# A two-layer hybrid block with routed experts: the modulation's sums as TensorE products, a table in longer runs, and new estimates for the planner

## The chip, the core and the metric

The kernel runs on one core of one Trainium2 chip. The metric is the time of one execution in device microseconds (us), as the median of the runs shown. The core has a matrix engine (TensorE, PE in the rows; PEld is its weight load), VectorE (DVE), ScalarE (ACT), GpSimd (POOL) and SyncE (SP), which issues the DMAs of this kernel in the order of its queue. Each engine takes its instructions in the order in which the program has them, and waits on semaphores for the others.

## The reference

One layer is computed for 512 latent tokens and 256 context tokens of 1024 channels: a bidirectional gated delta rule with 8 heads, whose context states seed the latent scans, and then an expert-choice mixture of 16 experts. Shift, scale and gate of both parts come from a modulation row.

```python
c_act = jax.nn.silu(c)
mod = c_act @ w_mod[i] + b_mod[i]
sh_m, sc_m, gt_m, sh_f, sc_f, gt_f = jnp.split(mod, 6, axis=-1)
u = modulate(rmsnorm(h, norm_mix_g[i]), sh_m, sc_m)
...
y, yc = gated_deltanet(u, uc, ...)       # projections, convolutions, chunked delta rule
h = h + gt_m * y
h = h + gt_f * ec_moe(modulate(rmsnorm(h, norm_ffn_g[i]), sh_f, sc_f), ...)
return rmsnorm(h, final_g)
```

## The kernel before

**The front** computes the norms, the modulation and the mixer; **the expert part** then streams 403 MB of expert weights (`wgu`, `wd`, `wdt`) through a ring of 2 MB tiles, each of which is used by products as it lands.

In the front, all channels of the tokens lie on partitions (`uh`, `ul` are the two halves of a split of the input, so that a projection takes three products instead of one, L141 to L143). `bulk` projects the 31 items (v, q, k, z of each head) one behind the other on TensorE. Each head then goes through these steps, of which different heads are in work at the same time:

- `conv` (L283): five taps on VectorE and ScalarE.
- `head_a`: reads the decay table from DRAM into two tiles `ff` (L1060), masks them on GpSimd (L1065), and builds the matrix of a chunk, whose diagonal blocks go through DRAM to `invert`.
- `invert`: 31 steps of two GpSimd instructions (L1148, L1150) that invert 32 x 32 blocks of all chunks; the blocks come in with `lb<-bd`, the result goes out with `xd<-xb` (L1153) and comes back with `cr<-xd` (L1158).
- `head_b`: puts the whole inverse together from the blocks, products from L1227 to L1275 with copies on VectorE between.
- `scan`: six steps in each of two directions, each a chain of products (L1315, L1321, L1333) and copies on VectorE and ScalarE. `decay_q` reads the table again for the queries (L1290).
- `head_o` and the output projection (L457 to L459): 64 sums of three products, 192 in all, of two heads together where they are paired, each closed by an addition into `hres` (L475). Router and top-k follow.

**The modulation** has two parts. The first sixteen column blocks are needed at the start and are products with `cst`, the activation padded to 32 columns (`mod_rows`, L818). The other 32 pieces of 512 KB (`mods`, `mod_piece`) are loaded one after the other into two slots (`e<-in_wm`, L344). A piece is multiplied by the activation and summed over eight blocks on VectorE (L373, L375), or on GpSimd (L355, L364, L367), or on ScalarE with sums on one of the others (L360, L364, L367), by the letters of `MOD_E`; then a product with a matrix of ones sums over the partitions (L382, L396).

**The table** `grow_d` is written once by `gates` as 96 rows of 128 values, a row for each direction, chunk and head, and read by `grow` with every partition reading the same rows: six of 512 bytes for `ff`, four for the queries.

**The order** of the front is written by a planner that runs when the program is built. Every step is a generator that asks for an engine with an estimated duration (`Ask("V", 0.25, t)`); the planner keeps a time for each engine, takes the request that could begin first (a rank decides between those that could begin together), and adds `HOP` before the next step may use the result. `dma` estimates loads. The estimates set only the order of the instructions; at run time an engine waits for what it needs. `E_AT` holds the first weights back until that planned time, `MOD_STEP` is the planned distance of two modulation pieces.

Of the kernel before, what the change touches and what calls it, by code (L numbers as in the profile page):

```python
# [25 lines left out]
H = 8  # L26
# [23 lines left out]
def gdn_moe_kernel(ctx: ExitStack, tc: tile.TileContext, a, out):  # L50
# [109 lines left out]
    def dma(nbytes, at=0.0):  # L160

        dq[0] = max(dq[0], at + 0.7) + nbytes / 360e3
        return dq[0] + 1.1
# [75 lines left out]
    av = lambda n_: 0.1 + n_ * 0.00084  # L239
    dv = lambda n_: 0.08 + n_ * 0.00104  # L240
# [17 lines left out]
    def conv(nm, h, n_, parts, last):  # L258
# [8 lines left out]
        else:  # L267
# [10 lines left out]
            for j in range(5):  # L278
                t = yield Ask("VA"[j == 0], 1.06 * dv(w) if j else 1.11 * av(w), t)
# [67 lines left out]
    def mod_piece(n_, j, wm, wsl, t):  # L347

        t = yield Ask(None, 0.0, lambda: t if n_ < 2 else None if ("mm", n_ - 2) not in done else max(t, done["mm", n_ - 2]))
        if MOD_E[n_] != "V":  # L350
            if MOD_E[n_] == "G":
                for i in range(2):
                    t = yield Ask("G", 1.25, t)
                    hk = slice(4 * i, 4 * i + 4)
                    g.tensor_tensor(wm[:, hk], wm[:, hk], cs1[:, hk, 0:1].to_broadcast([P, 4, P]), OP.mult)  # L355
            else:
                for i in range(4):
                    t = yield Ask("A", 0.59, t)
                    for k in (2 * i, 2 * i + 1):
                        s.mul(wm[:, k], wm[:, k], cs1[:, k, 0:1])  # L360
            en, on = ("V", v) if MOD_E[n_] == "B" else ("G", g)
            for i in (4, 2):
                t = yield Ask(en, dv(P * i) if en == "V" else 0.25 + 0.27 * i, t)
                on.tensor_add(wm[:, :i], wm[:, :i], wm[:, i:2 * i])  # L364
            t = yield Ask(en, dv(P) if en == "V" else 0.5, t)
            acc = accs[n_ % 2]
            on.tensor_add(acc, wm[:, 0], wm[:, 1])  # L367
        else:
            acc = accs[n_ % 2]
            for k in range(KT):  # L370
                t = yield Ask("V", 0.25, t)
                if k == 0:
# [133 lines left out]

    def with_router(hT, sl2, t, dst):

        t = yield Ask("P", 0.72, t, "pq")
        sl = take("pq")  # L510
        pr = psum_tile(ps, [P, P], "pq", 3)
        for k in range(KT):
# [1238 lines left out]
```

## Time and profile before

| what | us |
|---|---|
| median of 3 runs | 1574.14 |
| lowest and highest | 1568.88, 1575.66 |
| the profiled execution, its own time | 1573.24 |
| its span, first to last instruction | 1571.5 |
| TensorE busy in the span | 1374.7 (87%) |
| VectorE, ScalarE, GpSimd busy | 721.5, 405.3, 381.0 |
| mean granted share of TensorE's clock | 0.958 |

The profile is of one execution. The windows give busy time of each engine in a stretch, with the number of records in brackets; a 4-byte product of the kernel's kind stands in the records twice, so sixteen records are eight products. A wait is put down to what ended last before the waiting instruction began. The chain of waits is followed back from the last instruction.

### The profile page before, as it was taken

Reading aid. Unit: us, or ns where it says so; the run is one execution under the profiler, and the core shown is the slowest. Engines: PE = TensorE matmul, PEld = TensorE weight load, DVE = VectorE, ACT = ScalarE, POOL = GpSimd, SP = SyncE. Lnnn points to the kernel's source line nnn. Section 1 sums busy time; section 2 is a strip of 40 time slices with the busy share of each in tenths; the row PEclk is TensorE's granted clock in tenths of the full one; section 3 lists DMA queues with packets and bytes.
Section 4 is the critical chain, followed back from the end, with each engine's and each line's share of the span. In section 5 each row is a group of like instructions: output and inputs, shape, how many; then the busy total and the mean of one; then the engine's idle time right before and its main releaser. Section 6 shows DMA issues by size and latency. Waiting matters only on the chain.

```text
span 1571.5 us, 20699 instructions
## 1 busy us (share of the span) xinstructions
PE 1374.7 (87%) x8058; PEld 752.6 (48%) x8058; DVE 721.5 (46%) x1545; ACT 405.3 (26%) x1038; POOL 381.0 (24%) x645
## 2 busy tenths in 40 slices
PE   5889898988986889999999989889889899899867
PEld 1677687766875766433434324224223323324314
DVE  7779896977995896222222222222222222222103
ACT  3356474655574533000000000000000000000012
POOL 2548866857657830000000000000000000000001
PEclk8889999999998999999999999999999999999979
DMA  8145443443453566899999999999999999999992
GB/s 347 54 135 142 135 114 91 117 130 95 133 122 72 205 243 248 364 426 426 425 426 425 425 426 426 427 425 425 426 425 426 426 425 426 425 426 426 425 426 109
DMA packets 112515, 480.12 MB, mean 306 GB/s; under 512 B 45505, under 2 KB 66209, under 8 KB 81826
## 3 DMA queue, kind: packets, MB, share of 16 engines
q1 hardware_dynamic: 112418, 478.81, 77.9%
q8 instruction: 63, 1.03, 0.3%
q14 instruction: 34, 0.28, 0.1%
HBM read 471.92 MB, written 6.86 MB: 305 GB/s over the span
## 4 chain that ended last, share of the span: by engine, by line
DMA 48%; PE 26%; DVE 14%; POOL 8%; issue 2%; ACT 1%; SPq 0%; DVEq 0%; POOLq 0%; ACTq 0%
DMA w<-in_wgu 25%; DMA w<-in_wd 13%; PE gu L1580 10%; PE dn L1561 4%; POOL xb L1150 3%; POOL tb L1148 3%; DMA cr<-xd 2%; DVE e L375 2%; PE gc L1561 2%; PE gc L1511 2%; DMA fg<-in_fg 1%; DVE wl L303 1%; DMA ff__690<-grow_d 1%; DMA ff__1139<-grow_d 1%; PE gc L1548 1%
## 5 line engine op out<-in xcount | busy, mean ns | idle before, releaser
L1580 PE MATMUL gu<-w,xsT 128*64 128x512 f32 x2044 | 472.9, 606 | 32.4 <-DMA w<-in_wgu 31.6
L1580 PEld LDWEIGHTS gu<-w,xsT 128*64 128x64 f32 x2044 | 138.4, 138 | 291.5 <-issue 239.4
L1667 POOL TENSOR_TENSOR hres<-acc,fg 128x256 f32<-128x256 f32 (+1 forms) x6 | 6.0, 1004 | 953.1 <-DVE acc L1655 953.0
L1561 PE MATMUL dn<-w,work 128*64 128x512 f32 x896 | 202.0, 600 | 25.2 <-DMA w<-in_wd 25.2
L1550 DVE TENSOR_TENSOR acc<-gc,acc 128x512 f32<-128x512 f32 x104 | 70.7, 690 | 299.5 <-PE gc L1548 299.5
L141 PE MATMUL pp<-uh,wh 128*128 128x512 f32 (+1 forms) x368 | 153.4, 417 | 1.7 <-ACT cz L265 1.7
L143 PE MATMUL pp<-uh,wl 128*128 128x512 f32 (+1 forms) x368 | 138.9, 377 | 3.8 <-DVE wl L303 2.9
L142 PE MATMUL pp<-ul,wh 128*128 128x512 f32 (+1 forms) x368 | 137.9, 375 | 0.0
L1561 PEld LDWEIGHTS dn<-w,work 128*64 128x64 f32 x896 | 62.4, 137 | 154.2 <-issue 116.8
L1148 POOL TENSOR_TENSOR tb<-lb,xb 96x126 f32<-96x126 f32 (+22 forms) x248 | 118.3, 477 | 65.8 <-DMA lb<-bd 48.6
L1150 POOL TENSOR_TENSOR xb<-xb,tb 96x126 f32<-96x126 f32 (+22 forms) x248 | 125.1, 504 | 19.4
L1532 ACT ACTIVATE work<-tr 128x512 f32<-128x512 f32 x14 | 8.4, 597 | 423.1 <-PE tr L1525 423.1
L1512 DVE TENSOR_SCALAR xsT<-gc,ffn 128x128 f32<-128x128 f32 x64 | 26.2, 410 | 154.1 <-PE gc L1511 154.1
L1542 ACT CAST yh<-work 64x512 fp32r<-64x512 f32 x28 | 17.3, 617 | 253.1 <-DVE work L1539 252.8
L143 PEld LDWEIGHTS pp<-uh,wl 128*128 128x128 f32 x368 | 74.7, 203 | 16.1 <-DVE wl L303 3.3
L141 PEld LDWEIGHTS pp<-uh,wh 128*128 128x128 f32 x368 | 75.1, 204 | 10.7 <-ACT cz L265 2.2
L142 PEld LDWEIGHTS pp<-ul,wh 128*128 128x128 f32 x368 | 75.3, 205 | 6.3
L1511 PEld LDWEIGHTS gc<-oneh,hres 128*128 128x128 f32 x512 | 64.5, 191 | 20.2 <-issue 18.3
L1511 PE MATMUL gc<-oneh,hres 128*128 128x128 f32 x512 | 69.2, 280 | 0.4 <-DVE oneh L1504 0.4
L375 DVE SCALAR_TENSOR_TENSOR e<-e,cs,e 128x128 f32<-128x128 f32 x133 | 66.0, 512 | 1.8
L1613 DVE TENSOR_TENSOR work<-gu,work 128x512 f32<-128x512 f32 x32 | 22.0, 692 | 80.9 <-PE gu L1580 79.7
L1548 PEld LDWEIGHTS gc<-yh,pgt 128*128 128x128 f32 x112 | 19.8, 186 | 82.0 <-issue 68.2
(443 smaller groups left out, 2042.7 us busy)
## 6 DMA issues: line engine op xcount, KB each, us to landing
w<-in_wgu SPq DMA_DIRECT2D x100, 2048.0 KB, 34.3
w<-in_wd SPq DMA_DIRECT2D x45, 2048.0 KB, 34.3
w<-in_wgu SPq DMA_DIRECT2D x55, 1024.0 KB, 31.9
w<-in_wd SPq DMA_DIRECT2D x22, 1024.0 KB, 31.8
e<-in_wm SPq DMA_DIRECT2D x32, 512.0 KB, 4.4
wt<-in_win SPq DMA_DIRECT2D x31, 512.0 KB, 4.6
w<-in_wdt SPq DMA_DIRECT2D x6, 2048.0 KB, 30.7
wm<-in_wm SPq DMA_DIRECT2D x3, 2048.0 KB, 14.6
```

What stands on the lines that cost most here:

```text
L141: pe.matmul(pp, wh[:, k, :], uh[i][:, k, :], start=k == 0, stop=False)
L142: pe.matmul(pp, wh[:, k, :], ul[i][:, k, :], start=False, stop=False)
L143: pe.matmul(pp, wl[:, k, :], uh[i][:, k, :], start=False, stop=k == KT - 1)
L375: v.scalar_tensor_tensor(acc, wm[:, k], cs1[:, k, 0:1], acc, op0=OP.mult, op1=OP.add)
L1148: g.tensor_tensor(t_, lb[:, k + 1:, k:k + 1].to_broadcast([2 * NB, m, n_]), xb[:, k:k + 1, 0:n_].to_broadcast([2 * NB, m, n_]), OP.mult)
L1150: g.tensor_tensor(xb[:, k + 1:, 0:n_], xb[:, k + 1:, 0:n_], t_, OP.subtract)
L1511: pe.matmul(pg, hres[:, t, k * P:k * P + P], oneh[:, t].rearrange("p a b -> p (a b)"), start=t == 0, stop=t == NC_LAT - 1)
L1512: v.tensor_scalar(xsT[:, k, :], pg, ffn[:, 0, k:k + 1], ffn[:, 1, k:k + 1], op0=OP.mult, op1=OP.add)
L1548: pe.matmul(pcb, pgt[:, t, :], yh[:, dh], start=True, stop=True)
L1550: v.tensor_add(acc[t // 2][:, t % 2, cs], pcb, hres[:, t, cs] if first else acc[t // 2][:, t % 2, cs])
L1561: pe.matmul(pd[64 * g_:64 * g_ + 64], hs_[g_][i][:, cb, 64 * j:64 * j + 64], wcols(w, c0, w_), start=ft == 0, stop=ft == 15, tile_position ...
L1580: pe.matmul(gu[m][f // 2][hs], xsT[:, k, es], wcols(w, 2048 * m + 512 * f, 512), start=k == 0, stop=k == KT - 1, tile_position=(0, 64 * (f ...
```

## The change

Three things are changed.

1. **Modulation.** `MOD_E` goes. Each of the 32 pieces is now computed as the first sixteen blocks are: eight products with `cst`, four of them side by side in strips of 32 rows, into one PSUM tile; ScalarE copies it, and the closing product sums the four strips with `sel` (one column) or `selb` (the same column repeated). `cst` moves to a pool that lives through the front.
2. **Table.** `grow_d` has a row of 768 values for each direction and head. It is written with two DMAs and read with one run of 3 KB (for `ff`) or 2 KB (for the queries) per partition.
3. **Estimates.** Nearly every duration of the planner, `HOP`, the estimate of a DMA, `E_AT` and `MOD_STEP` get other values. The order of all five engines changes with them.

```diff
-    HOP = {"P": 0.27, "A": 0.33, "V": 0.33, "G": 0.35, "D": 0.0, None: 0.0}
+    HOP = {"P": 0.2, "A": 0.06, "V": 0.06, "G": 0.08, "D": 0.0, None: 0.0}
-    E_AT = (410, 425)
+    E_AT = (440, 460)
-    MOD_STEP = 7
-    MOD_E = "GGAGVVVVGVBVAVAVVVVVAVGAVVVVBVGV"
+    MOD_STEP = 11
-    def dma(nbytes, at=0.0):
-        dq[0] = max(dq[0], at + 0.7) + nbytes / 360e3
-        return dq[0] + 1.1
+    def dma(nbytes, at=0.0, more=0.0):
+        dq[0] = max(dq[0], at + 0.3) + nbytes / 380e3 + more
+        return dq[0] + 1.3
...
-                    t = yield Ask("G", 1.25, t)
-                    g.tensor_tensor(wm[:, hk], wm[:, hk], cs1[:, hk, 0:1].to_broadcast([P, 4, P]), OP.mult)
...
-            on.tensor_add(acc, wm[:, 0], wm[:, 1])
...
-                    v.scalar_tensor_tensor(acc, wm[:, k], cs1[:, k, 0:1], acc, op0=OP.mult, op1=OP.add)
-        give(wsl, t + 1.0)
+        t = yield Ask("P", 0.46, lambda: ..., "pq")
+        pm = psum_tile(ps, [P, P], "pq", 3)
+        for k in range(KT):
+            q = 32 * (k % 4)
+            pe.matmul(pm[q:q + 32, :], cst[:, k, :], wm[:, k, :], start=k < 4, stop=k >= 4)
+        give(wsl, t)
+        t = yield Ask("A", 0.27, t)
+        acc = accs[n_ % 2]
+        s.copy(acc, pm)
-        t = yield Ask("P", 0.15, t + 3.0, "pq")
+        t = yield Ask("P", 0.14, t, "pq")
-            pe.matmul(pc, acc, ones[:, 0:1], start=True, stop=True)
+            pe.matmul(pc, acc, sel[:, 0:1], start=True, stop=True)
-            pe.matmul(pb[hs], ones[:, hs], acc, start=True, stop=True)
+            pe.matmul(pb[hs], selb[:, hs], acc, start=True, stop=True)
...
-    grow_d = tc.dram_tile([2 * NCH * H, C], F32, name="grow_d")
+    grow_d = tc.dram_tile([2 * H, NCH * C], F32, name="grow_d")
-        sy.dma_start(grow_d, gr)
+        for d in range(2):
+            sy.dma_start(grow_d[d * H:(d + 1) * H].rearrange("h (c i) -> c h i", c=NCH), gr[d * NCH * H:(d + 1) * NCH * H])
-        return bass.AP(tensor=grow_d.tensor, offset=grow_d.offset + ((d * NCH + c) * H + h) * C,
-                       ap=[[0, P], [H * C, NCH - c], [1, C]])
+        return bass.AP(tensor=grow_d.tensor, offset=grow_d.offset + ((d * H + h) * NCH + c) * C,
+                       ap=[[0, P], [1, (NCH - c) * C]])
...
-                t = yield Ask("V", 0.26, t)
+                t = yield Ask("V", 0.335, t)
```

On TensorE a piece of modulation was one product amid the projections. A piece of the second quarter of the front, before (L382 is the closing product, L141 to L143 a projection's three):

```order
L142 MATMUL pp<-ul_112,wh 128x512
L143 MATMUL pp<-uh_110,wl 128x512
L382 MATMUL pq<-ones,e_455 128x1
L141 MATMUL pp<-uh_110,wh 128x512
L142 MATMUL pp<-ul_112,wh 128x512
L143 MATMUL pp<-uh_110,wl 128x512
```
And after (L353 are the eight products, L364 the closing one):

```order
L143 MATMUL pp<-uh_110,wl 128x512
L353 MATMUL pq<-e_449,cst 32x128 x8
L141 MATMUL pp<-uh_110,wh 128x512
L142 MATMUL pp<-ul_112,wh 128x512
L143 MATMUL pp<-uh_110,wl 128x512
L141 MATMUL pp<-uh_110,wh 128x512
L142 MATMUL pp<-ul_112,wh 128x512
L143 MATMUL pp<-uh_110,wl 128x512
L364 MATMUL pq<-sel,e_450 128x1
L141 MATMUL pp<-uh_110,wh 128x512
```
The eight products have come in, and six products of a projection stand between them and the closing product, which waits for ScalarE's copy.

On GpSimd, the end of the first inversion and the start of the second, before (L355 to L367 are a piece of modulation):

```order
L1148 TENSOR_TENSOR tb<-lb,xb 96x16
L1150 TENSOR_TENSOR xb<-xb,tb 96x16
L355 TENSOR_TENSOR e_454<-e_454,cs_117 128x512 x2
L364 TENSOR_TENSOR e_454<-e_454 128x512
L364 TENSOR_TENSOR e_454<-e_454 128x256
L367 TENSOR_TENSOR e_455<-e_454 128x128
L1141 MEMSET xb 96x512
L1142 COPY xb<-par 96x16x2
L1148 TENSOR_TENSOR tb<-lb,xb 96x31
L1150 TENSOR_TENSOR xb<-xb,tb 96x31
```
And after:

```order
L1134 TENSOR_TENSOR tb<-lb,xb 96x16
L1136 TENSOR_TENSOR xb<-xb,tb 96x16
L1127 MEMSET xb 96x512
L1128 COPY xb<-par 96x16x2
L1134 TENSOR_TENSOR tb<-lb,xb 96x31
L1136 TENSOR_TENSOR xb<-xb,tb 96x31
```
The piece between the two inversions is gone.

On TensorE in the last head's scan (L1315, L1321 and L1333 are a step's three products, L457 to L459 the output projection), before:

```order
L1315 MATMUL sc_6217<-wa,ya 128x128
L1315 MATMUL sc_6221<-wa,ya 128x128
L501 MATMUL pq<-wrp,ones 128x32
L457 MATMUL pp<-woh,oh 128x512
L458 MATMUL pp<-woh,ol 128x512
L459 MATMUL pp<-wol,oh 128x512
L1321 MATMUL sc_6217<-R,ua 128x128
L1321 MATMUL sc_6221<-R,ua 128x128
L457 MATMUL pp<-woh,oh 128x512
L458 MATMUL pp<-woh,ol 128x512
L459 MATMUL pp<-wol,oh 128x512
L1333 MATMUL sc_6217<-Vs,qa 128x128
```
And after (a step is L1301, L1307, L1319; L496 and L519, L506 are products and transposes of the router):

```order
L1307 MATMUL sc_6353<-vx,ua 128x128
L1307 MATMUL sc_6361<-vx,ua 128x128
L1319 MATMUL sc_6353<-Vs,qa 128x128
L1319 MATMUL sc_6361<-Vs,qa 128x128
L496 MATMUL pq<-hT,wr 32x128 x8
L1301 MATMUL sc_6381<-wa,ya 128x128
L1301 MATMUL sc_6383<-wa,ya 128x128
L519 MATMUL pq<-ident,hres 128x128 x4
L1307 MATMUL sc_6381<-R,ua 128x128
L506 MATMUL pq<-selr,rs 128x16
L1307 MATMUL sc_6383<-R,ua 128x128
L1319 MATMUL sc_6381<-Vs,qa 128x128
```
The output projection has left the scan. Ahead of the last head's L1227 (now L1213) stood 78 of its 192 products, and 132 stand there now; the 256 new products of modulation stand ahead of it as well.

## Rows read from the trace of the kernel before

**Rows 1.** Windows: stretch, its length, busy us (records) per engine, clock, DMA share, GB/s.

```profile
0.00:40.00 40.00, 21.00 (x82) 8.20 (x82) 27.94 (x64) 14.35 (x24) 10.27 (x17) 0.83 0.87 341
40.00:105.00 65.00, 53.20 (x294) 44.58 (x292) 44.58 (x78) 29.80 (x72) 36.60 (x34) 0.84 0.27 86
105.00:557.00 452.00, 387.63 (x3091) 324.84 (x3090) 371.32 (x820) 265.66 (x740) 319.63 (x581) 0.93 0.47 124
557.00:617.00 60.00, 54.28 (x502) 43.65 (x501) 48.82 (x109) 21.55 (x58) 8.49 (x7) 1.00 0.76 295
617.00:633.00 16.00, 15.18 (x45) 6.82 (x43) 10.56 (x40) 3.58 (x8) 0.00 (x0) 1.00 0.10 43
633.00:1537.00 904.00, 819.68 (x3821) 307.80 (x3822) 203.89 (x408) 62.19 (x113) 0.00 (x0) 0.98 1.01 424
```
**Rows 2.** Chain of waits in the expert part: start us, us, what.

```profile
...
908.56 34.34 DMA w<-in_wd
942.96 34.32 DMA w<-in_wgu
...
```
**Rows 3.** Chain of waits between 40 and 557 us, shares of that stretch.

```profile
by line: POOL xb L1150 10.4%; POOL tb L1148 9.4%; DMA cr<-xd 6.2%; DVE e L375 6.1%; issue 5.5%; DVE wl L303 2.8%; DMA ff__690<-grow_d 2.8%; DMA ff__1139<-grow_d 2.6%; DMA ff__3654<-grow_d 2.5%; DMA e<-in_wm 2.2%; DMA xd<-xb 2.2%; DMA ff__23
...
```
**Rows 4.** TensorE's waits, 40 to 557 us: us in total, times, longest.

```profile
PE pq L1227 <- DVE cx L1218: 18.9, 4, 8.5
PE pq L382 <- POOL e L367: 8.7, 2, 4.4
...
PE pq L396 <- POOL e L367: 3.2, 1, 3.2
...
```
**Rows 5.** Groups by line, 40 to 520 us: busy us, mean ns | idle before.

```profile
L1148 POOL TENSOR_TENSOR tb<-lb,xb 96x126 f32<-96x126 f32 (+22 forms) x229 | 109.1, 476 | 64.5 <-DMA lb<-bd 48.6
L364 POOL TENSOR_TENSOR e<-e 128x512 f32<-128x512 f32 (+1 forms) x22 | 23.4, 1065 | 1.1
L355 POOL TENSOR_TENSOR e<-e,cs 128x512 f32<-128x512 f32 x12 | 14.7, 1240 | 0.0
...
L375 DVE SCALAR_TENSOR_TENSOR e<-e,cs,e 128x128 f32<-128x128 f32 x133 | 66.0, 512 | 1.8
L373 DVE TENSOR_SCALAR e<-e,cs 128x128 f32<-128x128 f32 x19 | 6.7, 352 | 4.0 <-DMA e<-in_wm 4.0
...
L360 ACT ACTIVATE e<-e,cs 128x128 f32<-128x128 f32 x56 | 18.5, 397 | 1.5 <-DMA e<-in_wm 1.5
```
**Rows 6.** Timelines of TensorE and of ScalarE: start us, us, what.

```profile
576.32 0.39 PE L457 MATMUL pp<-woh,oh 128*128 128x512 f32 x1
576.55 0.39 PE L458 MATMUL pp<-woh,ol 128*128 128x512 f32 x1
...
594.65 0.64 PE L514 MATMUL pq<-hT,wr 128*32 128x128 f32 x16
595.22 0.71 PE L1321 MATMUL sc<-R,ua 128*128 128x128 f32 x4
...
595.36 0.27 ACT L519 COPY rs<-pq 128x128 f32<-128x128 f32 x1 [2.88 <-PE pq L514]
```
**Rows 7.** Landing of the loads of L344, L1060 and L1290, in this order.

```profile
DMA to landing us min/median/max: 3.1/4.4/11.9
...
DMA to landing us min/median/max: 7.2/9.3/14.3
...
DMA to landing us min/median/max: 6.4/8.6/10.8
```
**Rows 8.** SyncE's waits in its queue, 40 to 520 us: us, times, longest.

```profile
SPq L1153 <- POOL xb L1150: 99.4, 7, 28.9
SPq L344 <- DVE e L375: 37.4, 9, 9.2
```
**Rows 9.** Windows around one of TensorE's waits, columns as in rows 1.

```profile
375.20:380.20 5.00, 0.05 (x1) 0.00 (x0) 0.41 (x2) 0.00 (x0) 4.92 (x7) 1.00 0.70 93
380.30:387.00 6.70, 6.03 (x112) 5.06 (x112) 6.45 (x19) 2.38 (x11) 3.26 (x11) 0.50 0.90 302
```

More of the change, by code (lines that the diff above doesn't have):

```diff
@@ L237, in run @@
             on_step()
[L239 to L240 removed]
+    av = lambda n_: 0.14 + n_ * 0.00088
+    dv = lambda n_: 0.15 + n_ * 0.00104
     nh = H
@@ L347, in mod_piece @@
     def mod_piece(n_, j, wm, wsl, t):
[L349 to L352, printed above, removed]
-                    t = yield Ask("G", 1.25, t)
-                    hk = slice(4 * i, 4 * i + 4)
-                    g.tensor_tensor(wm[:, hk], wm[:, hk], cs1[:, hk, 0:1].to_broadcast([P, 4, P]), OP.mult)
[L356 to L366, printed above, removed]
-            on.tensor_add(acc, wm[:, 0], wm[:, 1])
[L368 to L372, printed above, removed]
-                    v.tensor_scalar(acc, wm[:, k], cs1[:, k, 0:1], None, op0=OP.mult)
-                else:
-                    v.scalar_tensor_tensor(acc, wm[:, k], cs1[:, k, 0:1], acc, op0=OP.mult, op1=OP.add)
-        give(wsl, t + 1.0)
+        t = yield Ask("P", 0.46, lambda: t if n_ < 2 else None if ("mm", n_ - 2) not in done else max(t, done["mm", n_ - 2]), "pq")
+        sl = take("pq")
+        pm = psum_tile(ps, [P, P], "pq", 3)
[6 more added lines that the diff above has]
+        s.copy(acc, pm)
+        give(sl, t)
         b1 = slice(16 + j, 17 + j)
-        t = yield Ask("P", 0.15, t + 3.0, "pq")
+        t = yield Ask("P", 0.14, t, "pq")
         sl = take("pq")
@@ L407, in first_projections @@
                 for i in range(2):
[L408 removed]
+                    t = yield Ask("P", ((0.46, 0.24), (0.70, 0.36))[j][i] * (1 if k > 2 else 1.5), lambda: None if ("w", j - 2) not in done or ("u", k) not in done else max(done["w", j - 2], done["u", k]), None if k else tags[j][i])
                     if k == 0:
@@ L450, in bulk @@
                 for h in hs:
-                    t = yield Ask("P", 0.67, lambda: fin(*((w_, h) for h in hs for w_ in (f"wow{hf}", "woo"))), "pp" if h == hs[0] else None)
+                    t = yield Ask("P", 0.77, lambda: fin(*((w_, h) for h in hs for w_ in (f"wow{hf}", "woo"))), "pp" if h == hs[0] else None)
                     if h == hs[0]:
@@ L572, in route_l @@
     def route_l():
-        t = yield Ask("P", 0.85, lambda: fin(("w7", 0), ("O", nh - 1), *(("lg", i) for i in range(NC_LAT))), "pq")
+        t = yield Ask("P", 0.8, lambda: fin(("w7", 0), ("O", nh - 1), *(("lg", i) for i in range(NC_LAT))), "pq")
         sl = take("pq")
@@ L721, in out_w @@
         tl = tail.get("tl")
-        t = yield Ask("G", 1.25, lambda: None if fin(*(("M", j) for j in range(8))) is None else max(t, *(done["M", j] for j in range(8))))
+        t = yield Ask("G", 1.31, lambda: None if fin(*(("M", j) for j in range(8))) is None else max(t, *(done["M", j] for j in range(8))))
         g.tensor_mul(wt, wt, gtm[:, 512 * hf:512 * hf + 512])
@@ L772, in gdn_moe_kernel @@
     act("silu", cs1, cc, AF.Silu)
+    cst = up.tile([P, KT, 32], F32)
+    v.memset(cst, 0.0)
+    v.tensor_copy(cst[:, :, 0:2], cs1)
+    selb = up.tile([P, P], F32)
+    v.tensor_copy(selb, sel[:, 0:1].to_broadcast([P, P]))
     tbl["kind"] = table["kind"] = "exp"
@@ L776, in gdn_moe_kernel @@
     with tc.tile_pool(name="st", bufs=1, side="right") as st:
-        cst = st.tile([P, KT, 32], F32, name="cst")
-        v.memset(cst, 0.0)
-        v.tensor_copy(cst[:, :, 0:2], cs1)
         xs_ = [st.tile([P, KT, n], F32, name=f"x{i}") for i, n in enumerate((SEQ, CTX))]
@@ L1079, in head_a @@
             give(sl, max(t, t2))
-        t = yield Ask("A", 0.25, t, table="exp")
+        t = yield Ask("A", 0.54, t, table="exp")
         lnk = ga.tile([P, NCH], F32, tag="lnk", bufs=1, name="lnk")
@@ L1098, in head_a @@
             for i in range(2):
-                t = yield Ask("A", 0.85, tv, table="exp")
+                t = yield Ask("A", 0.975, tv, table="exp")
                 for c in range(3 * i, 3 * i + 3):
```

145 lines of the change are left out of this document (72 added, 73 removed).

## The prediction

> **What bounds the kernel now.** I read the stages first, then the end of the chain of waits, then TensorE's waits. The windows [rows 1] cut the run at 617 us, where the last scan, the output projection and the router's products end, at 633 us, where the expert part begins, and at 1537 us, where the weights end. From 633 to 1537 us the DMA share is 1.01 at 424 GB/s, and the chain there is one weight load after another, 34.34 us each [rows 2]. The expert part takes its time from bytes that the change doesn't touch. So it starts earlier or later with the front, and whatever the front gains or loses passes through one for one, as long as the tiles that are fetched ahead have landed: DMA moves only 43 GB/s in the 16 us before 633 [rows 1], so they have some 10 us in hand, against about 5 us for a 2 MB tile at 424 GB/s.
>
> So the question is what 617 us become. TensorE's busy time is the largest there: 21.0 + 53.2 + 387.6 + 54.3 = 516.1 of 617 us [rows 1], 100.9 us idle, of which 19.0 in the first 40 us, 76.2 between 40 and 557, and 5.7 after. 557 us is where the last head's block inverse reaches TensorE. The chain of waits between 40 and 557 us runs through other engines, though [rows 3]: the inversions on GpSimd (10.4% and 9.4% of 517 us), the modulation on VectorE (L375, 6.1%), its loads (2.2%), the return of the inverse (6.2%), and the table's loads, of which the three longest alone have 7.9%. The list of TensorE's waits [rows 4] shows the same from its side: 18.9 us for the inverse (L1227), 11.9 us for modulation sums (8.7 + 3.2), the rest in small hops to VectorE. The front is two things almost in balance: a chain outside TensorE that is longer, and a TensorE that is full to 84% and has little to give.
>
> **Modulation moves to TensorE.** What goes: 66.0 us of VectorE in 133 instructions (and the 19 that begin each piece), 14.7 + 23.4 us of GpSimd, 18.5 us of ScalarE [rows 5]. What comes, per piece: eight products with 32 rows of result each, a copy on ScalarE, and the same closing product as before. The router's products have exactly that shape: they start at 594.65 and the next product starts at 595.22, so eight take 0.57 us; the copy behind them takes 0.27 us [rows 6]. 32 pieces cost TensorE 32 x 0.57 = **18.2 us** and ScalarE 8.6 us, half of what leaves it. All of the 18.2 lies on the engine that is fullest, none of it is hidden.
>
> The waits change too. The 11.9 us for modulation sums end. In their place TensorE itself stands until a piece's load has landed and until ScalarE has copied. No row shows that wait; it is bounded below by 0 (the order puts other products between the two, six in the piece that the section on the change shows) and above by the whole gap between the load time that the planner counts for 512 KB (0.3 + 1.38 + 1.3 = 2.98 us, the formula in the diff) and the 4.4 us median of the row [rows 7], 32 x 1.4 = 45 us. I take 5 us, near the low end: SyncE issues a load as soon as the slot is free, and only 5.5 us of waits on these loads stand in the rows of before (4.0 and 1.5, [rows 5]).
>
> **The queue of SyncE.** A load of modulation waits in order on SyncE until its slot has been read, 37.4 us for L375 alone [rows 8], and tables, projection weights and the inverse's return are queued behind. TensorE frees the slot 0.57 us after it has begun. This is a gain of the chain, not counted by itself. The larger wait of SyncE, 99.4 us for the inversion's last row before it is written out [rows 8], stays.
>
> **GpSimd and the inversions.** Without the pieces nothing stands between one inversion and the next but masks and the decayed queries. About 38 us leave GpSimd over eight heads, 4.8 us a head, and VectorE, which makes an inversion's input and takes its output, has 73 us less in 517. TensorE's 18.9 us for the inverse should fall to about 4, and of the other 45 us of small waits (76.2 - 18.9 - 11.9) I keep two thirds, 30: together **30 us** saved. The bounds: 10, if the inversions wait for their input all the same (GpSimd waited 48.6 us for it, [rows 5]), and 50.
>
> **The table in long runs.** A head's load of the table brings a partition six runs of 512 bytes now (four for the queries), and one run of 3 or 2 KB after. The 384 KB load lands in 7.2 to 14.3 us, median 9.3, the 256 KB load in 8.6; the 512 KB load with 4 KB per partition lands in 4.4 [rows 7]. I take the last row's price for the new loads, about 4 us, and so 5 us less on each of two loads a head. On the chain the three longest loads alone take 41 us (7.9% of 517, [rows 3]), and more than half of that would go; but what it shortens is the same wait of TensorE for the inverse that is counted above, so it gets no term of its own. I put a third of the 30 us on it, 10.
>
> The Trainium skill says in "DMA: Bandwidth & Descriptors", section Specifications, that 512 bytes is already the smallest transfer for line rate. By that rule the runs of 512 bytes lose nothing, and the sum would be without those 10 us. The rows speak against it: fewer bytes in 512-byte runs take twice the time of more bytes in long runs. It is rival 3 below.
>
> **The estimates.** With them the planner writes another order. The one place where this can be priced is the end: 132 instead of 78 of the 192 output products stand ahead of the last head's inverse on TensorE, and between the steps of the last scan there are none (the order in the section on the change). At 0.23 us a product (start to start, [rows 6]) that is 12.5 us moved forward, neither added nor taken. After 557 us the last head's chain, which now waits behind these products step by step, sets the time; TensorE has 54.3 - 12.5 = 41.8 us of work there, and I give the chain 55 us instead of 60. So idle time grows by 13.2 - 5.7 = **7.5 us** at the end. The rest of the new order I count at nothing; its bounds are in the range.
>
> **The clock.** The granted clock is 0.84 from 40 to 105 us and 0.93 to 557 [rows 1]. Its levels are 1.2 and 2.4 GHz, so 65 x 0.32 + 452 x 0.14 = 84 us run at the low one, at most 42 us of TensorE's work lost. The rows show one fall and what came before it: 5 us in which TensorE was busy 0.05 us, waiting for the inverse, then 6.7 us at 0.50 [rows 9]. With less than half of the idle time left I take a third of the 42 back, **14 us**, bounds 0 and 30.
>
> **Sum.** +18.2 (products) - 11.9 + 5 (modulation's waits) - 30 (inverse and hops) + 7.5 (end) - 14 (clock) = -25.2 us. The front ends at 592 instead of 617. The profiled execution took 1573.24 us around a span of 1571.5, and the median of the three runs is 1574.14, 0.9 above it; I predict from the profiled one: 1573.2 - 25.2 = **1548 us**.
>
> **Rivals.**
> 1. *TensorE hardly waits any more.* The chain outside it loses 32 + 11 us of modulation and over 20 of loads, more than TensorE's 76 us of idle time minus 18 of new work. Then the savings of 30 become 50 and the clock gives 25 to 30: 18.2 - 6.9 - 50 + 7.5 - 27 = -58, 1515 us. For it: the chain of waits. Against: small hops of a scan don't depend on modulation.
> 2. *TensorE stands on modulation's loads and copies (slower).* TensorE takes its work in order, so a load that is late by 1.4 us stops projections and scans alike. Price up to 45 us instead of 5, without the clock's gain (more idle spells): 1548 + 40 + 14 = 1602; at half of that, 1575 to 1580. It decides from about 1.0 us a piece, where 32 us eat the gain. For it: the closing product comes soon behind its copy, and pieces are put in front of projections. Against: the few waits on these loads before.
> 3. *The long runs don't speed up the table.* 10 us of the 30 stay: 1558.
> 4. *One bottleneck in place of another.* The savings are 12 instead of 30 and the clock gives 4, since GpSimd still waits for its input: 1573 + 18.2 - 6.9 - 12 + 7.5 - 4 = 1576, no change that can be measured.
> 5. *The new order works against the end (slower).* 54 more products stand ahead of the last inverse. If its input is ready at 557 all the same, 12.5 + 18.2 us of TensorE work are late in the critical place and nothing has been saved: 1588 or so.
>
> **How the numbers follow.** The forecast has 0.52 with its own range 1532 to 1563, which includes rival 3; rival 1 has 0.18; rival 4 has 0.15; rivals 2 and 5 have 0.10 and 0.05. About 0.5% is what a measurement of this kernel can tell from no change, some 8 us: faster means below 1566, slower above 1582. Faster 0.52 + 0.18 = 0.70 and 0.02 of rival 4: 0.72; same 0.13; slower 0.15. The range leaves out nearly half of rival 1 and most of rivals 2 and 5: 1516 to 1580.
>
> **What would show it.** The expert part must have the same length, from the first weight's product to the end, within 2 us. In the front: TensorE busy about 520 of 592 us; the waits on L1227 (now L1213) near 4 us; no row of TensorE's waits for the new line of eight products or for the closing one above 5 us in all; table loads near 4 us; the clock above 0.95 between 105 and the end of the front. The prediction is wrong if waits for modulation on TensorE reach 20 us, if GpSimd still waits some 50 us for its input with TensorE waiting behind, or if the expert part doesn't follow the front.

## The result: 0.9% faster, and the profile after

The changed kernel took 1558.72 us as the median of seven runs (1553.8 to 1564.09), beside 1572.16 us of the kernel before; the ratio is 0.9909, with an interval of 0.9889 to 0.9928. That is 13.4 us less, where 25 were forecast (1548) in a range of 1516 to 1580. The span of the profiled execution went from 1571.5 to 1557.0 us.

The windows of the changed kernel are cut where its stages end: at 545 us the last head's inverse reaches TensorE, at 603 the output projection ends, at 621.9 the first weight's product begins. Columns as in [rows 1].

```profile
0.00:40.00 40.00, 21.20 (x110) 8.60 (x114) 28.47 (x67) 15.43 (x25) 6.23 (x15) 0.84 0.88 341
40.00:105.00 65.00, 63.41 (x404) 51.66 (x396) 44.44 (x85) 30.98 (x71) 21.66 (x21) 0.92 0.30 99
105.00:460.00 355.00, 328.57 (x3048) 274.54 (x3044) 256.31 (x545) 218.70 (x610) 236.42 (x454) 0.97 0.42 127
460.00:505.00 45.00, 28.94 (x279) 24.65 (x279) 29.86 (x73) 30.53 (x80) 27.18 (x50) 0.73 0.57 175
505.00:545.00 40.00, 38.21 (x202) 30.80 (x200) 30.49 (x65) 12.78 (x33) 30.52 (x54) 1.00 0.47 143
545.00:603.00 58.00, 50.32 (x445) 38.62 (x445) 35.00 (x81) 18.66 (x51) 2.12 (x3) 0.88 0.65 250
...
621.90:1557.00 935.10, 842.18 (x4044) 323.42 (x4044) 216.15 (x428) 70.39 (x140) 5.98 (x6) 0.98 0.98 413
```

And the kernel before, from its first weight's product on:

```profile
635.80:1571.50 935.70, 841.55 (x4044) 323.28 (x4044) 216.21 (x428) 70.39 (x140) 5.98 (x6) 0.98 0.98 412
```

The expert part has the same length, 935.1 and 935.7 us; the whole gain was made in the front, which ends at 603 instead of 617 us. TensorE was busy for 21.2 + 63.4 + 328.6 + 28.9 + 38.2 + 50.3 = 530.7 of these 603 us and idle for 72.3, where it was busy for 516.1 and idle for 100.9 before [rows 1]. One stretch stands out: from 460 to 505 us it was busy for 28.9 of 45 us at a granted clock of 0.73.

TensorE's longest waits from 40 to 557 us, which answer to [rows 4]:

```profile
PE sc L1319 <- DVE vx L1316: 8.1, 7, 1.8
PE pq L353 <- DMA e<-in_wm: 7.9, 2, 6.0
PE pq L1027 <- ACT vx L1188: 6.1, 1, 6.1
...
PE pq L1213 <- DVE cx L1204: 2.2, 1, 2.2
```

The 18.9 us for the inverse have become 2.2 (L1213), the 11.9 us for modulation sums are gone, and 7.9 us for modulation's loads have come (L353). The table's loads, L1046 for `ff` and L1276 for the queries, which answer to [rows 7]:

```profile
DMA to landing us min/median/max: 4.0/5.3/6.8
...
DMA to landing us min/median/max: 3.4/4.8/6.6
```

### The profile page after: what moved, and what is told of

Same layout as the page of the kernel before. It is cut to its first block, busy times and chain, and to the rows that moved or that the text cites. A ratio compares the mean times of both kernels' runs of the same rounds, so it can differ in the third digit from the quotient of the medians.

```text
span 1557.0 us, 21526 instructions
## 1 busy us (share of the span) xinstructions
PE 1389.3 (89%) x8570; PEld 760.2 (49%) x8570; DVE 653.3 (42%) x1388; ACT 401.2 (26%) x1016; POOL 330.1 (21%) x600
## 2 busy tenths in 40 slices
DMA packets 96129, 480.17 MB, mean 308 GB/s; under 512 B 45501, under 2 KB 45725, under 8 KB 65438
## 4 chain that ended last, share of the span: by engine, by line
DMA 36%; PE 29%; DVE 3%; ACT 1%; issue 1%; POOL 0%; DVEq 0%; SPq 0%; ACTq 0%; POOLq 0%
DMA w<-in_wgu 21%; DMA w<-in_wd 13%; PE gu L1566 12%; PE dn L1547 5%; PE gc L1497 2%; PE gc L1547 2%; DMA fg<-in_fg 1%; PE gc L1534 1%; PE pp L439 1%; PE pp L441 1%; PE pp L440 1%; PE sc L1319 1%; PE sc L1307 1%; DMA wot<-in_wo 0%; PE sc L1301 0%
## 5 line engine op out<-in xcount | busy, mean ns | idle before, releaser
L141 PE MATMUL pp<-uh,wh 128*128 128x512 f32 (+1 forms) x368 | 148.8, 404 | 5.3 <-ACT pad L272 5.3
L143 PE MATMUL pp<-uh,wl 128*128 128x512 f32 (+1 forms) x368 | 134.1, 364 | 0.3 <-DVE wl L302 0.2
L142 PE MATMUL pp<-ul,wh 128*128 128x512 f32 (+1 forms) x368 | 133.6, 363 | 0.0
L1136 POOL TENSOR_TENSOR xb<-xb,tb 96x126 f32<-96x126 f32 (+22 forms) x248 | 119.0, 480 | 19.4
L1498 DVE TENSOR_SCALAR xsT<-gc,ffn 128x128 f32<-128x128 f32 x64 | 26.2, 409 | 153.5 <-PE gc L1497 153.5
L141 PEld LDWEIGHTS pp<-uh,wh 128*128 128x128 f32 x368 | 71.9, 195 | 17.9 <-issue 5.7
L143 PEld LDWEIGHTS pp<-uh,wl 128*128 128x128 f32 x368 | 71.1, 193 | 12.1 <-DVE wl L302 0.6
L142 PEld LDWEIGHTS pp<-ul,wh 128*128 128x128 f32 x368 | 71.9, 195 | 6.0
L1534 PE MATMUL gc<-yh,pgt 128*128 128x512 f32 x112 | 52.3, 487 | 7.7 <-DVE acc L1536 7.7
## 6 DMA issues: line engine op xcount, KB each, us to landing
w<-in_wgu SPq DMA_DIRECT2D x55, 1024.0 KB, 31.9
w<-in_wd SPq DMA_DIRECT2D x22, 1024.0 KB, 31.9
w<-in_wdt SPq DMA_DIRECT2D x6, 2048.0 KB, 31.9
wm<-in_wm SPq DMA_DIRECT2D x3, 2048.0 KB, 13.1
```

The source lines that it names most:

```text
L141: pe.matmul(pp, wh[:, k, :], uh[i][:, k, :], start=k == 0, stop=False)
L142: pe.matmul(pp, wh[:, k, :], ul[i][:, k, :], start=False, stop=False)
L143: pe.matmul(pp, wl[:, k, :], uh[i][:, k, :], start=False, stop=k == KT - 1)
L1136: g.tensor_tensor(xb[:, k + 1:, 0:n_], xb[:, k + 1:, 0:n_], t_, OP.subtract)
L1498: v.tensor_scalar(xsT[:, k, :], pg, ffn[:, 0, k:k + 1], ffn[:, 1, k:k + 1], op0=OP.mult, op1=OP.add)
L1534: pe.matmul(pcb, pgt[:, t, :], yh[:, dh], start=True, stop=True)
```

## The three parts apart

Since the change has three parts, I ran every combination of them: the long runs of the table (T), modulation on TensorE (M) and the estimates (E). Theory by then: TensorE's idle time is what is won, and modulation wins most of it. The rivals are that one of the other two carries the gain.

| kernel | median us | ratio to before | interval |
|---|---|---|---|
| T, first run | 1553.0 | 0.9877 | 0.9862 to 0.9892 |
| M, second run | 1585.9 | 1.0088 | 1.0055 to 1.0122 |
| E, third run | 1632.8 | 1.0388 | 1.0371 to 1.0405 |
| M and T, fourth run | 1554.0 | 0.9886 | 0.9871 to 0.9901 |
| M and E, fifth run | 1582.2 | 1.0059 | 1.0038 to 1.0080 |
| T and E, sixth run | 1601.7 | 1.0169 | 1.0131 to 1.0207 |
| all, the change | 1558.7 | 0.9909 | 0.9889 to 0.9928 |

The runs come from several sessions, in which the kernel before took between 1571.3 and 1576.0 us; each ratio goes by the kernel before of its own session, and differences of medians between sessions carry these few us.

**First run: the table alone.** The estimates and the order of the instructions are those of before; only the one DMA that writes the table has become two.

```diff
-    grow_d = tc.dram_tile([2 * NCH * H, C], F32, name="grow_d")
+    grow_d = tc.dram_tile([2 * H, NCH * C], F32, name="grow_d")
-        return bass.AP(..., ap=[[0, P], [H * C, NCH - c], [1, C]])
+        return bass.AP(..., ap=[[0, P], [1, (NCH - c) * C]])
```

> The kernel before with the table in long runs and nothing else: instructions and their order as before. Prediction's term: the loads of the table fall from 9.3 and 8.6 us to about 4 to 5, and a third of the 30 us of TensorE's waits goes with them, 10 us: 1562. Rival a (the table carries the whole gain of the change): 1558. Rival b (the loads are fast but hidden, or 512-byte runs lose nothing): 1572, within 4 us of the kernel before.

It gained 20.5 us, more than the whole change and more than the theory or either rival had said. The loads of `ff` and of the queries landed in

```profile
DMA to landing us min/median/max: 3.9/4.9/5.4
...
DMA to landing us min/median/max: 5.6/5.7/5.9
```

instead of 9.3 and 8.6 [rows 7]. Why that is worth so much shows in the list of who waited for the `ff` loads, here of the kernel before (us, times):

```profile
  POOL ff__3654 L1065: 5.5, 1
  POOL ff__3596 L1065: 5.2, 1
  POOL ff__690 L1065: 5.1, 1
  POOL ff__660 L1065: 3.7, 1
  POOL ff__4343 L1065: 2.5, 1
...
```

GpSimd, which also does the inversions, stood 28.0 us in front of the masks, in nine places. In the first run two such waits are left:

```profile
  POOL ff__3655 L1067: 1.0, 1
  POOL ff__3597 L1067: 0.4, 1
```

The inverse of each head reached TensorE earlier, by an amount that grew up to the seventh head: at 160.9 instead of 165.0 us for the first head, at 310.9 instead of 322.4 for the fourth, at 483.4 instead of 505.6 for the seventh, at 540.0 instead of 558.2 for the last. Waits of ScalarE for loads fell in the same run, for the queries' table from 14.6 to 0.5 us and for projection weights (L299) from 26.2 to 13.1. So the layout of the table is shown to carry the 20.5 us; how they divide among GpSimd's waits and these was not run apart.

**Second run: modulation alone.** `mod_piece`, `MOD_STEP` and `cst` of the change, the rest of before.

```diff
-            for k in range(KT):
-                t = yield Ask("V", 0.25, t)
-                ... v.scalar_tensor_tensor(acc, wm[:, k], cs1[:, k, 0:1], acc, ...)
+        for k in range(KT):
+            q = 32 * (k % 4)
+            pe.matmul(pm[q:q + 32, :], cst[:, k, :], wm[:, k, :], start=k < 4, stop=k >= 4)
```

> The kernel before with modulation on TensorE alone, table and estimates as before. Theory (TensorE's idle time is traded for its work): TensorE gets 18.6 us of products and its idle time up to the last output product falls by more than 20 us: 1566 to 1570. Rival a (the estimates carry the gain, modulation only costs): the 18.6 us stand on the path, 1585 to 1591. Rival b (modulation carries everything): 1558.

It was 0.9% slower, which is rival a's time. Up to the first weight's product TensorE was busy for 549.7 us, 16.6 more than before, and idle for 97.6 us, only 5.0 less. The longest of its waits:

```profile
PE pq L353 <- DMA e<-in_wm: 38.6, 9, 6.8
```

The eight products stood 38.6 us for their loads, which were queued with the table's slow ones (they landed in up to 14.6 us, median 4.9; in the fourth run, where the order is the same and only the table differs, in up to 9.0, median 4.7). This is the prediction's second rival, in a kernel in which the table was not changed: bounded there by 45 us, it came to 38.6.

**Third run: the estimates alone.**

```diff
-    HOP = {"P": 0.27, "A": 0.33, "V": 0.33, "G": 0.35, "D": 0.0, None: 0.0}
-    E_AT = (410, 425)
+    HOP = {"P": 0.2, "A": 0.06, "V": 0.06, "G": 0.08, "D": 0.0, None: 0.0}
+    E_AT = (440, 460)
...
-                t = yield Ask("V", 0.26, t)
+                t = yield Ask("V", 0.335, t)
```

> The kernel before with the new estimates, the transfers' price, HOP and the two prefetch times, but with modulation on the old engines and the table in short runs. Theory: an order of work can only close gaps that the chain through VectorE and GpSimd leaves, 1568 to 1574. Rival a (the estimates carry the gain): 1555 to 1560. Rival b (they fit only the changed kernel, and the early preparation of output weights holds up the last heads as in the changed kernel): 1576 to 1585.

It was 59 us slower, beyond every case that I had named. The longest waits of TensorE from 500 to 620 us, and those of GpSimd from 500 to 680:

```profile
PE pq L396 <- DVE e L375: 9.2, 1, 9.2
PE pq L396 <- DVE e L367: 7.2, 1, 7.2
```

```profile
POOL wot L723 <- DMA wot<-in_wo: 56.0, 9, 20.0
...
POOL wot L723 <- DVE gtm L398: 5.8, 1, 5.8
```

In the order that the planner wrote from the new durations, the pieces of modulation come late: the gate's last sum was added at 574.6 us (506.6 before), and only then could the output weights be multiplied by it. They have one of the lowest ranks on VectorE and GpSimd (7, where the inversion has 6); that this rank put them there is read from the planner and was not run apart. TensorE had no output products to do meanwhile; the first weight's product began at 694.8 us.

**Fourth to sixth run: two parts each.**

```diff
 fourth:  second run + the table
 fifth:   the change - the table (grow, grow_d and its loads as before)
 sixth:   the change - modulation (mod_piece, MOD_E, MOD_STEP as before)
```

> Modulation on TensorE and the table in long runs, with the estimates of before. Theory: the two help the same wait for the inverse, so that they add up to less than their sum, 1558 to 1564. Rival a (the estimates carry the gain): 1575 to 1590. If it comes under 1555, the new estimates cost time in the changed kernel.

> The changed kernel with the table in short runs again. Theory after the first runs (the long runs carry the gain, alone 20.5 us): the loads take 9 us again and the changed kernel loses about those 20 us: 1575 to 1582. Rival a (modulation and estimates carry a gain of their own that doesn't need the table): 1562 to 1567. Rival b (the new order asks for the table so early that slow loads are hidden): 1557 to 1561.

> The changed kernel with modulation on the old engines. Theory: with the longer estimates the planner puts the pieces of modulation, which have the lowest rank on VectorE and GpSimd, to the end (in the run of the estimates alone the last sum of the gate is added at 574.6 us, against 506.6 before), and the output weights wait for it: 1590 to 1620. Rival (the table cures that too, since the inversions come earlier): 1553 to 1560.

With the table in long runs, modulation on TensorE costs nothing that can be measured: 1554.0 beside 1553.0 us. The theory of the fourth run, 1558 to 1564, fell. Its waits for loads there are 14.8 us instead of 38.6:

```profile
PE pq L353 <- DMA e<-in_wm: 14.8, 4, 6.2
```

Windows from the start to the first weight's product show what was exchanged, here of the kernel before, the first run, the fourth run and the changed kernel:

```profile
0.00:635.75 635.75, 533.11 (x4014) 429.27 (x4014) 505.34 (x1117) 334.94 (x898) 374.99 (x639) 0.92 0.50 148
0.00:616.20 616.20, 527.57 (x4014) 426.30 (x4014) 519.06 (x1117) 334.68 (x898) 376.75 (x639) 0.94 0.47 153
0.00:617.20 617.20, 538.84 (x4526) 432.72 (x4526) 438.61 (x960) 327.56 (x876) 328.72 (x594) 0.95 0.47 153
0.00:621.90 621.90, 547.12 (x4526) 436.76 (x4526) 437.18 (x960) 330.83 (x876) 324.12 (x594) 0.93 0.47 152
```

The table alone took TensorE's idle time from 102.6 to 88.6 us and, with a higher granted clock, its busy time from 533.1 to 527.6. Modulation beside it made TensorE busy for 11.3 us more and idle for 10.2 us less. The new estimates, with the same products, took another 3.6 us of idle time but let it be busy for 8.3 us more, at a granted clock of 0.93 instead of 0.95.

Taking the table's runs back out of the changed kernel costs 23.4 us (fifth run, at the upper end of the theory after the first runs). Taking modulation back costs 43 us (sixth run), by the mechanism of the third: the gate's last sum at 544.4 us, against 459.6 in the changed kernel. So the table gains 20 to 32 us in each of the four pairs (20.5 alone, 31.9 beside modulation, 31.1 beside the estimates, 23.4 beside both), and in each pair the order of the instructions is the same. Modulation gains only beside the new estimates, which need it. The new estimates themselves bring nothing beside the other two: 1554.0 us without them, 1558.7 with them, and the intervals overlap.

## Is TensorE the bound?

**Seventh run: the eight products twice**, in the same order.

```diff
-        for k in range(KT):
+        for k in (*range(KT), *range(KT)):
```

> The changed kernel with the eight products of each piece done twice, so 32 x 0.58 = 18.6 us more work on TensorE and the same order. Theory (TensorE is the bound of the front): all of it shows, 1575 to 1580. Rival a (half of it falls into gaps where TensorE waits for a load or another engine): 1566 to 1570. Rival b (the chain outside TensorE is the bound): 1559 to 1562.

It took 1560.62 us, ratio 0.9919 (0.9892 to 0.9947): 18.6 us more work cost about 2 us, less than the intervals can tell from none. The time of my theory fell, and rival b gave the right one. The windows, cut as above (the last inverse is used at 547 here):

```profile
40.00:105.00 65.00, 63.38 (x489) 52.05 (x486) 43.55 (x88) 31.90 (x73) 22.19 (x21) 0.96 0.31 102
105.00:460.00 355.00, 333.96 (x3463) 281.45 (x3463) 256.25 (x542) 216.80 (x602) 235.14 (x455) 0.99 0.42 126
460.00:505.00 45.00, 28.49 (x281) 24.22 (x280) 31.66 (x75) 30.96 (x85) 24.67 (x43) 0.73 0.53 153
505.00:547.00 42.00, 40.65 (x224) 32.11 (x226) 31.75 (x65) 14.02 (x36) 32.82 (x59) 1.00 0.51 160
547.00:603.00 56.00, 48.08 (x443) 37.22 (x442) 34.37 (x81) 18.57 (x51) 1.90 (x3) 0.91 0.65 247
```

Busy time from 40 to 603 us is 514.6 against 509.5: only 5.1 of the 18.6 us show, and they came out of idle time. Most of the rest was paid by the clock, which was granted at 0.96 and 0.99 up to 460 us instead of 0.92 and 0.97: by these shares 65 x 0.16 + 355 x 0.06 = 32 us ran at the low level without the double work and 12 with it, and 20 us less at half speed are, as an estimate, some 10 us of work. In this run work in idle time kept the clock up, and the work behind it then took less. Since TensorE became busy for only 5 us longer, the run does not settle whether TensorE, busy for 392 of the 420 us up to 460, bounds the changed kernel there. Against it speaks that the heads' inverses reached it at nearly the same times with the double work (213.3 instead of 215.0 us for the second head, 432.0 instead of 431.5 for the sixth).

## The hole between 474 and 502 us

The stretch at a clock of 0.73 is where the missing part of the forecast was to be looked for. Its windows in the changed kernel:

```profile
475.00:480.00 5.00, 0.00 (x0) 0.00 (x0) 3.82 (x8) 2.49 (x12) 1.36 (x1) 0.76 1.02 331
480.00:485.00 5.00, 2.08 (x52) 1.59 (x52) 2.48 (x8) 4.64 (x17) 0.00 (x0) 0.50 0.70 122
485.00:490.00 5.00, 3.29 (x77) 3.04 (x76) 4.79 (x13) 4.80 (x13) 3.46 (x3) 0.50 0.97 275
490.00:495.00 5.00, 1.28 (x18) 0.91 (x18) 4.76 (x6) 2.68 (x7) 4.64 (x8) 0.50 0.13 34
```

TensorE had done all projections and had no output products yet. It waited from 474.6 us on for ScalarE (L1188), which the order had put behind copies of output weights (L715), and these waited for GpSimd and for their loads. ScalarE's waits from 460 to 505 us have that, and SyncE's timeline shows what else was queued:

```profile
ACT woh L715 <- POOL wot L705: 3.9, 3, 2.4
```

```profile
470.36 0.49 SPq L653 DMA_DIRECT2D hres<-in_xt  x1
470.95 0.63 SPq L659 DMA_DIRECT2D wr<-in_wr  x1
472.68 5.31 SPq L1144 DMA_DIRECT2D cr<-xd  x1
478.09 4.48 SPq L1276 DMA_DIRECT2D qa<-grow_d  x2
482.67 0.38 SPq L1114 DMA_DIRECT2D bd<-cd  x1
483.10 3.44 SPq L698 DMA_DIRECT2D wot<-in_wo  x3
488.21 0.80 SPq L1123 DMA_DIRECT2D lb<-bd  x2
```

The last head's blocks were ready at 475.8 us, went out at 482.7, and their loads were issued at 488.2 behind three output weights. The last inversion began at 494.0. It ended at 536.1: three more products with output weights (L705), waits for their loads, and two products with the queries' table (L1284) stood within it. GpSimd's waits for these loads from 493.5 to 536.5 us:

```profile
POOL wot L705 <- DMA wot<-in_wo: 4.3, 2, 2.9
```

**Eighth run: output weights at a lower rank.**

```diff
-    RANK = {..., "out": 5, ...}
+    RANK = {..., "out": 7, ...}
-        launch(6, tail_loads(t))
+        launch(8, tail_loads(t))
```

> The changed kernel with the preparation of the output weights given a lower rank, so that on ScalarE the copies for the last head stand ahead of it. Theory (the hole of 474 to 502 us, with 24 us at the low clock, comes from these steps standing ahead of the last head's on ScalarE and on the DMA queue): the last inversion starts some 8 us earlier, 1545 to 1551. Rival (the hole only moves, since TensorE has run out of projections and the output products now come later): 1557 to 1565.

1545.92 us (1542.88 to 1547.86), ratio 0.9823 (0.9794 to 0.9852), as the theory had it and the fastest kernel of the study: it beats both the kernel before and the changed one, and the interval lies clear of the changed kernel's. The last inversion began at 484.8 us, 9.2 us earlier, and the first weight's product at 607.4 instead of 621.9. The earlier start, on which the theory went, is only a part of it: nothing stands within the inversion now, so that it took 30.8 us (to 515.6) instead of 42.1, and its result reached TensorE at 530.1 instead of 545.1. The hole became smaller but did not go:

```profile
476.00:496.00 20.00, 12.41 (x162) 9.45 (x163) 16.76 (x31) 9.37 (x20) 15.39 (x28) 0.50 0.49 137
```

**Ninth run: the 2 MB of the residual stream behind the last inversion's loads.**

```diff
-        t = yield Ask("D", 0.5, t)
-        sy.dma_start(tail["hres"], ...)        # ahead of wr
+        t = yield Ask("D", 0.5, t + 16.0)
+        sy.dma_start(tail["hres"], ...)        # behind wr
```

> The kernel of the eighth run with the 2 MB load of the residual stream moved behind the loads for the last head's inversion. In that run the return of head 6's inverse took 9 us from issue to use (465.4 to 474.8), behind the 2 MB issued at 463.6, and the input of the last inversion was ready at 470.7 but issued at 475.8. Theory (what is left of the hole is this one transfer ahead of two small ones): the last inversion starts some 8 us earlier, 1535 to 1541. Rival (TensorE then waits for the residual stream, or the transfers that it is now ahead of pay for it): 1544 to 1550.

The last inversion began 4.1 us earlier (480.7) and its result was used 6.5 us earlier (523.6 instead of 530.1), but the first weight's product came 5 us later (612.4), and the time was 1550.18 us, ratio 0.9864 (0.9842 to 0.9886). That is the rival's time, at its upper end; the interval overlaps a little with the eighth run's, so a loss against it is hardly shown, but the gain did not come. What was gained ahead of the last scan was lost behind it. Where exactly was not settled; one wait of 5.0 us of TensorE for the router's copy (L506 for L501) is new there.

**Tenth run: the estimates of before with the lower rank**, that is the fourth run with the edit of the eighth.

```diff
 fourth run, with "out": 7 and launch(8, tail_loads(t))
```

> Modulation on TensorE and the table in long runs with the estimates of before (the fourth run), and with the lower rank of the output weights of the eighth. It shows what the new estimates are worth once that rank is the same. In the fourth run the last inversion began at 463.4, 30 us earlier than in the changed kernel, and was held up to 531.6 by six products with the output weights on GpSimd. Theory (they were what it was held up by): 68 us become about 45, and the end comes earlier than in the fourth run, 1535 to 1548, as good as with the new estimates. Rival (TensorE then has no output products to do while the last inverse runs, and the work is only moved behind it): 1550 to 1558.

1564.6 us, ratio 0.9950 (0.9932 to 0.9968): slower than the fourth run. The expectation rested on a misreading. At 463.4 us only the inversion's clearing of its tile began; its first step ran at 485.9, so the inversion had taken 45 us and not 68, with 10.2 of them for eight products with output weights (six on `wot`, two on staging tiles). In the tenth run it took 34.0 us, and the last inverse reached TensorE at 533.7 us instead of 543.4. But TensorE had no output products up to 525.8 us, where the fourth run began with them at 506.0 (it was busy for 20.85 of 40 us from 505 to 545, against 31.80 in the fourth run). So the work was only moved behind the last inverse, as the rival had it, at a time beyond the rival's own. The lower rank is worth 13 us with the new estimates and costs 10 with the old ones: a rank that helps in one order need not help in another.

**Eleventh and twelfth run: the hole filled.** The eighth run with 80 products into a tile that nobody reads, and the same with the eight products twice.

```diff
+        if h == nh - 2:
+            pd = psum_tile(ps, [P, 512], "pp", 2)
+            for _ in range(36):
+                pe.matmul(pd[:, :P], ident, ident, start=True, stop=True)
         py = psum_tile(ps, [P, NCH, 32], "pq", 3)
...
```

> The kernel of the eighth run with 80 products of a constant with itself, into a tile that nobody reads, where TensorE waits for the inverse of head 6 (36, 14, 24 and 6 ahead of the four steps, at 0.11 us each 4.0, 1.5, 2.6 and 0.7 us, against gaps of 4.2, 2.0, 3.2 us). In the eighth run the granted clock is 0.50 from 476 to 496 us, and some 24 output products run at 0.43 instead of 0.23 us there. Theory (what lowers the clock is the idle spell, and the clock sets the time): the granted clock of 475 to 497 us is 1.00 and the kernel some 4 us faster, 1539 to 1543. Rival a (the last inversion on GpSimd sets the end, TensorE's clock there doesn't matter): clock 1.00 and 1544 to 1548. Rival b (the added products are late in front of the steps): 1549 or more.

> The same with the eight products of each piece of modulation done twice. In the changed kernel this added 18.6 us of TensorE's work at full clock and cost 2 us, while the time at the low clock between 40 and 640 us fell from 69 to 46 us. Theory (work that is put into idle time pays for itself with the clock): within 4 us of the eleventh run. Rival (the eleventh kernel has less idle time to give, so that the work shows): 8 to 19 us slower than the eleventh run.

The eleventh took 1552.06 us, ratio 0.9854 (0.9832 to 0.9877). Its windows:

```profile
476.00:480.00 4.00, 4.00 (x38) 4.00 (x38) 3.14 (x9) 1.94 (x10) 2.25 (x2) 1.00 0.76 195
...
496.00:500.00 4.00, 2.41 (x7) 2.03 (x8) 4.00 (x7) 0.00 (x0) 3.61 (x6) 0.53 0.00 0
```

The clock stayed at 1.00 up to 496 us, where it was 0.50 from 476 on in the eighth run; so it was the idle spell that had lowered it. But the added products were too long, as TensorE's timeline shows:

```profile
473.69 8.20 PE L1212 MATMUL pp<-ident 128*128 128x128 f32 x72
481.83 0.62 PE L1217 MATMUL pq<-cx,ct 32*32 32x32 f32 x48
```

36 products are 72 records and took 8.2 us, not the 4.0 that I had put in by counting a record as a product. The next step began 5.8 us later than in the eighth run, and the clock fell behind them anyway. That is rival b, by its time too, though the interval overlaps with the eighth run's, so that a loss against it is not shown. What the clock alone is worth in this hole stays open; it was not tried with half the products. The twelfth took 1558.70 us, ratio 0.9889 (0.9870 to 0.9909), 6.6 us more than the eleventh, between what theory and rival had said. The two intervals overlap a little. That a part of the work shows here because less idle time was left fits, but was not shown by itself.

## Why the prediction came out as it did

**The stages: right.** The expert part didn't move (0.6 us), and the front's gain of 14 us passed through one for one.

**The products' price: right; that none of it would be hidden: wrong.** 0.57 us for eight was forecast from the router's; the timeline has 0.58, from their start to the next product's:

```profile
172.53 0.64 PE L353 MATMUL pq<-e,cst 128*32 128x128 f32 x16
173.11 0.50 PE L141 MATMUL pp<-uh,wh 128*128 128x512 f32 x1
```

But beside the table the whole move to TensorE cost about 1 us, no more than the intervals can tell from none (fourth run against the first), and the same products a second time about 2 (seventh run).

**Idle time: right as a sum.** 100.9 - 11.9 + 5 - 30 + 7.5 = 71.5 us were forecast, 72.3 were measured. The wait for the inverse fell to 2.2 us (4 forecast), modulation's own waits came to 7.9 + 0.8 = 8.7 with those for the copy (L364; 5 forecast, and L353's 7.9 are over the 5 that it named as a sign), and the idle time at the end grew from 5.7 to 58 - 50.3 = 7.7 us (13.2 forecast). That the sum came out is in part luck, since the 30 us were not won where the prediction put them (below).

**The clock: the term of the sum that was mis-sized.** Busy time should have been 516.1 + 18.2 - 14 = 520.3 us; it was 530.7. With the 18.6 us that the products took, the clock gave back 516.1 + 18.6 - 530.7 = 4 us instead of 14, and that is 10 of the 11 us by which the forecast missed. The prediction took idle time as the measure. By the windows, some 84 us ran at the low level up to 557 us before; in the changed kernel it is 65 x 0.16 + 355 x 0.06 + 45 x 0.54 + 58 x 0.24 = 70 us, and 24 of them lie in the one hole. 14 us less at half speed are 7 us of work as an estimate, also short of the forecast's 14. Idle time had fallen by more than a quarter, but a part of what was left had gathered in one place. The loss comes with the new estimates: with the same products in the order of before (fourth run) TensorE was busy for 8.3 us less up to the first weight's product. The sign that the prediction named, a clock above 0.95 from 105 us on, failed in just these windows (0.73 and 0.88).

**Where the 30 us come from: wrong.** The prediction gave them to modulation's leaving VectorE and GpSimd, and a third to the table. The first run shows that the table alone gains 20.5 us, and the fourth that modulation adds nothing to it with the estimates of before. The step that failed is "what it shortens is the same wait of TensorE for the inverse that is counted above, so it gets no term of its own". The loads held up GpSimd in nine places, 28.0 us in all, and every inverse came later with them. That list could have been read before; I had added up TensorE's waits and SyncE's, and of GpSimd's only those for the inversions' input. So what was priced at 10 of the 30 us gained 20.5 alone, more than the whole change. That the time still came out near the forecast is luck in so far as this gain covered what the other two parts did not bring.

The Trainium skill says in "DMA: Bandwidth & Descriptors", section Specifications, that 512 bytes are already enough for line rate. The first run speaks against it for this load: the same 384 KB, in runs of 3 KB instead of 512 bytes, land in 4.9 us instead of 9.3. The change also made the six runs of a partition neighbours in DRAM, where they had lain 4 KB apart, and the two were not run apart. For this load the measurement decides, and rival 3 of the prediction (1558) is refuted as a mechanism, although its number is the one that came out.

**The second rival was real.** TensorE would have stood 38.6 us for modulation's loads (second run); the long runs took that away (14.8 in the fourth run, 7.9 in the changed kernel). The two parts that I had costed separately depended on each other through the loads.

**The estimates: counting them at nothing was wrong.** Alone they cost 59 us, beside the table 49, beside modulation they change nothing that the intervals can tell (4 us less), and beside both they cost between nothing and 5. The place that I priced, the end, was the wrong one: the idle time came at the point where projections run out and output products can't begin yet.

## What to carry to other kernels

Price a load by who stands behind it: add up its waits on every engine that works in order, not only on the busiest. Run the parts of a compound change apart, in all combinations if there are three: here one part carried the whole gain, one was good only beside another, and new estimates made the kernel 59 us slower as long as modulation stayed on engines where its pieces came last. Look for the place where one kind of work runs out before the next can start; idle time that gathers there costs the clock as well.

## What the runs showed of the hardware

Doing 32 x 8 products twice, 18.6 us at the high clock, cost about 2 us in the changed kernel: the granted clock rose from 0.92 and 0.97 to 0.96 and 0.99 in the two windows where they were added, and 5 us came out of idle time. In the twelfth run, with the hole filled, the same came to 6.6 us more, with intervals that overlap a little. And a read in which every partition takes the same rows got faster when its runs of 512 bytes, 4 KB apart, became one run: from 9.3 to 4.9 us for 384 KB and from 8.6 to 5.7 us for 256 KB (medians, first run). The page of the profile counts the packets: 112515 before and 96129 after for the same 480 MB, as the 16 x 128 x 10 runs (directions and heads, partitions, six and four runs) have become 16 x 128 x 2.

```profile
DMA packets 96129, 480.17 MB, mean 308 GB/s; under 512 B 45501, under 2 KB 45725, under 8 KB 65438
```
